# The first two weight sums of a seven-product matrix product: a VectorE addition against a plain load and an accumulating DMA

## Chip, core and metric

The kernel runs on one core of a Trainium2 chip. The metric is device time in microseconds (us): the median of several runs of the whole program. The engines are named as in the profile: PE (TensorE, matrix products; PEld are its weight loads), DVE (VectorE), ACT (ScalarE), POOL (GpSimd) and SP (SyncE, which here only issues DMAs). Weights, inputs and outputs lie in HBM; all work is done on tiles in SBUF, and products land in PSUM.

## What is computed

One inference step of a two-layer decoder trunk, for 512 prompt tokens and 8 x 4 sample tokens, 544 columns in all, with 1024 model channels. Every layer adds a token mixer and then a gated ConvFFN to the residual stream:

```python
for i in range(DEPTH):                       # 2 layers
    h = rms_norm(x, norm_mix[i])
    x = x + (conformer_conv if i == 0 else stick_breaking_attention)(h)
    h = rms_norm(x, norm_ffn[i])
    g = h @ w_gate                           # 1024 -> 2816
    g_conv = causal_dwconv(concat(past, g), w_dw, b_dw)      # width 3
    x = x + (silu(g_conv) * (h @ w_up)) @ w_down             # 2816 -> 1024
y = rms_norm(x, norm_final)
```

All inputs and outputs are float32. The change concerns weight matrices of 1024 rows, of which 256 columns are handled at a time: those of `w_gate` and `w_up` outside the first pass of each FFN, and half of the query matrix.

## The kernel before

**Products.** Each float32 product is made of three products of rounded operands: a weight tile W is split into a high half `whi` (ACT, L397, a cast) and a low half `wlo` (DVE, L400, W minus the high half); the data are split likewise into `XH` and `XL`. PE then adds whi x XH, whi x XL and wlo x XH in PSUM.

**Weights.** A raw tile (`raw`, 128 x 8 x 256 float32, 1 MB) holds 256 columns of a weight matrix: 8 blocks of 128 rows. There are two raw buffers; the load of the next but one is issued on SP (from the twelfth raw tile on; L360) as soon as the last split that reads the old one is emitted. The split pairs are kept in five slots (`SPLIT_BUFS`): slot s is written over slot s - 5, so a split can begin once PE is done with the fifth slot before it.

**Seven products for eight.** A "quad" is a raw tile seen as a 2 x 2 matrix of blocks of 512 rows x 128 columns, A11, A21 (the second 128 columns of the first 512 rows), A12 and A22, in the kernel's own naming; with the data also cut in two halves of 272 columns, seven block products and some additions give what eight would (Strassen's scheme in Winograd's form). It takes four slots, of kind 0, 2, 3 and 4: the plain first columns; the two sums in tile S; the third and fourth sums, which L1367 and L1369 write over the raw tile; and one plain block. `S[:, 0]` is A21 + A11 and `S[:, 1]` is A21 + A22: the two sums that this case is about. L1367 makes the third sum from `S[:, 1]`. Each of the seven block products is 12 matmuls of 128 x 272 (`products`, L1604 on). The data's own four sums are tiles TH and TL; `inputs` (L1460 on) makes them at the start of each FFN and uses the memory of S as scratch.

**S.** There is one S buffer per FFN (`pools["S"]`, L1448) and one for the query matrix (L1841). `sums` (L1353) takes it from a ring of one, so that a new pair of sums may be written only when every reader of the old pair is done: the high split, the low split, and L1367. 36 quads lie in the two FFNs, 2 in the query matrix.

**Order of the work.** Each FFN is planned as a whole: `plan.op` notes operations with an engine, an estimated cost and what they read (r) and write (w); `Plan.run` (L191) then simulates the engines and emits each engine's instructions in the order in which the simulation starts them. The emitted order is fixed; at run time each engine goes through its instructions in order and waits on semaphores. An operation on an engine name that does not exist (such as `raw5`) emits nothing and only holds back what depends on it, which is how the landing of a DMA is modelled. `used(slot)` (L1377) is called when the products of a slot are planned; it plans the split of the slot five further on, and, where that slot is of kind 2, the sums of its raw tile first.

**The FFN's passes.** The 22 chunks of 128 hidden channels go in passes of 4, 6, 6 and 6. The first pass is made of plain products. In each later pass come three gate quads with a down projection (the pass before, L1710) after each, the remaining down projections, and three up quads one behind the other; the first gate quad of the next pass follows at once. Gate products are copied (ACT, L1661) or added (DVE, L1666) into a tile G, whose columns for the samples' history POOL copies beforehand (L1541); POOL also copies the new state out of G (L1573, L1574) and issues its stores (L1728). L1564 is the convolution's multiply-add on DVE, L1716 the down projection's addition to the residual xT, L1865 and L1867 the evaluation of query quads. L2017 gathers cache pages by indirect DMA on POOL: 128 rows of 1024 float32 each.

Of the kernel before, what the change touches and what calls it, by code (L numbers as in the profile page):

```python
# [14 lines left out]
ALU = mybir.AluOpType  # L15
PSUM = bass.MemoryType.PSUM

P = 128
# [32 lines left out]
H_BUFS = 4  # L51
ACC_LATE = 5.5
U_POST = 1.0

WARM = (17, 29)
WARM_URGENT = 2.5
# [193 lines left out]
def tile_trunk(  # L250
# [8 lines left out]
    nc = tc.nc  # L259
    dve, act, pool, pe = nc.vector, nc.scalar, nc.gpsimd, nc.tensor  # L260
# [20 lines left out]
    raws = []  # L281
# [134 lines left out]
    W = Ring()  # L416
# [43 lines left out]
    def bank(tag, name):  # L460
        if tag == "tr" and "one" in banks:
            turns[0] += 1
            tag = "tr" if turns[0] % 3 else "one"
        return ps.tile([P, 512], F32, tag=tag, name=name, bufs=banks[tag])
# [3 lines left out]
    def uid(s):  # L468
        _n[0] += 1
        return f"{s}_{_n[0]}"  # L470
# [17 lines left out]
    def gemm(pt, st, slot, xh, xl, places=None, ks=(0, NF)):  # L488

        hi, lo, nk = W.w[slot]  # L490
        c0, n = st
        o = pt[:, :n]
        for k in range(max(0, ks[0]), min(nk, ks[1])):
            pe.matmul(o, hi[:, k, :], xh[:, k, c0:c0 + n], start=(k == 0), stop=False)
            pe.matmul(o, hi[:, k, :], xl[:, k, c0:c0 + n], start=False, stop=False)
            pe.matmul(o, lo[:, k, :], xh[:, k, c0:c0 + n], start=False, stop=(k == nk - 1))
            if places is not None and (k + 1) * 4 // nk > k * 4 // nk:
                for f in places[k * 4 // nk]:
                    f()
# [9 lines left out]
    def begin(n, ready, s0, st, xh, xl):  # L509

        pts = [bank("acc", uid("acc")) for _ in range(n)]
        for i, pt in enumerate(pts):
            gemm(pt, st, s0 + i, xh, xl, None, (0, ready))
        return pts
# [193 lines left out]
    for i in range(2):  # L708
        ch0 = (PE_CHUNKS[0] + i * len(PE_CHUNKS) // 2) * P
        for m in range(8):  # L710
            nj = min(4, CW - 4 * m)
            pool.dma_start(out=trow[i][m * n_g:(m + 1) * n_g, :nj * 32].rearrange("g (j h) -> g j h", j=nj),
                          in_=conv_w_dw[0, 4 * m:4 * m + nj, ch0:ch0 + n_g * 32].rearrange("j (g h) -> g j h", h=32))
# [4 lines left out]
    plan = Plan(E_CONV, 0.12, CONV_SHIFTS)  # L718
# [246 lines left out]
    blocks = [(xr[b], P, b) for b in range(4)] + [(xs, NS, 4)]  # L965
# [137 lines left out]
    for c in range(0, NC, 2):  # L1103
# [9 lines left out]
        for cc in range(2):  # L1113
            plan.op("act", 0.33, lambda c=c, cc=cc, pt=pt: act.copy(
                ext_s[:, c + cc, :, 0:PAST], pt()[:, cc * 240:(cc + 1) * 240].rearrange("p (b t) -> p b t", b=NB)),
                r=[pt, "junk"], w=[("past", c + cc)])
# [124 lines left out]
    for h, (c0, n) in enumerate(STREAMS):  # L1241
        if h:
            layer_norm(1)
        for g in (0, 4):
            for i in range(4):
                c = g + i
                pt = product(s0 + c, h)
                x = xT[:, c, c0:c0 + n]
# [3 lines left out]
        if not h:  # L1252
# [8 lines left out]
            r=[nrm.acc[0]], w=[ms])  # L1261
    plan.op("act", 0.34, lambda: act.activation(rs()[:, :n], ms()[:, :n], AF.Sqrt, bias=eps_t[:, 0:1], scale=1.0),
            r=[ms, "table"], w=[rs])
    plan.op("dve", 1.7, lambda: dve.reciprocal(rs()[:, :n], rs()[:, :n]), w=[rs])
    for c in range(NC):
# [3 lines left out]
                r=[rs, ("x", c, 0)], w=[u])  # L1269
# [4 lines left out]
            r=[u, ("XH", c, 0)], w=[("XL", c, 0)], lift=NLIFT)  # L1274
# [26 lines left out]
    def ffn(l, before, after):  # L1301
# [9 lines left out]
        plan = Plan(E_FFN)  # L1311
# [23 lines left out]
        def dcost(n):  # L1335
            return 0.06 + n * 1.06e-3

        def acost(n):
            return 0.04 + n * 0.885e-3
# [13 lines left out]
        def sums(r):  # L1353

            S = plan.tile("S", 1, lambda: pools["S"])
            S.after |= pools["inputs"]
            first = ("slot", s_of[r])

            def pair():
                x, s = W.raw[r], W.sums  # L1360
                s[r] = S()
                blocks = bass.AP(x.tensor, x.offset, [list(x.ap[0]), [4 * 2 * P + P, 2], [2 * P, 4], [1, P]])
                a21 = x[:, 0:4, P:]
                dve.tensor_tensor(S(), a21[:, None].to_broadcast([P, 2, 4, P]), blocks, op=ALU.add)

            plan.op("dve", dcost(1024), pair, r=[("raw", r)], w=[S])
            plan.op("dve", dcost(512), lambda: dve.tensor_tensor(  # L1367
                W.raw[r][:, 0:4, 0:P], S()[:, 1], W.raw[r][:, 0:4, 0:P], op=ALU.add), r=[("raw", r), S, first], w=[("S2", r)])
            plan.op("dve", dcost(512), lambda: dve.tensor_tensor(  # L1369
                W.raw[r][:, 4:, 0:P], W.raw[r][:, 0:4, 0:P], W.raw[r][:, 4:, 0:P], op=ALU.add), r=[first], w=[("S2", r)])  # L1370
            return S
# [5 lines left out]
        def used(slot):  # L1377

            s = slot + SPLIT_BUFS
            if ends and slot >= ends[0]:  # L1380
                if ends[0] + SPLIT_BUFS <= slot < ends[0] + NC:
                    return
                if slot < ends[0] + SPLIT_BUFS:
                    s = slot + NC
            if s >= len(specs):
                return
            r, kind, last, nk = specs[s]
            if kind == 0:
                s_of[r] = s
            if kind == 2:  # L1390
                live[r] = sums(r)
            prepare(s, [("slot", slot)])
# [160 lines left out]
        def smp(x, m, n):  # L1553
            return x[:, m:n].rearrange("p (b i) -> p b i", b=NB)
# [22 lines left out]
        def plain_pair(f2, s0, k0):  # L1577
# [16 lines left out]
            for i in range(2):  # L1594
# [3 lines left out]
                for c0, n in (SA, SB):  # L1598
                    plan.op("dve", dcost(n), lambda c0=c0, n=n, pt=ups[i, (c0, n)], h=h, s=sil[f]: dve.tensor_tensor(
                        h()[:, c0:c0 + n], s()[:, c0:c0 + n], pt()[:, :n], op=ALU.mult), r=[ups[i, (c0, n)], sil[f]], a=[h],  # L1600
                        urgent=U_POST)
                low_h(f, k0, h)
# [48 lines left out]
        def gate_quad(f2, slots):  # L1651
            g = [G(f2 + i) for i in range(2)]

            def put(what, p):
# [5 lines left out]
                if what[0] == "keep" or what[0] == "12":  # L1660
                    plan.op("act", acost(m), lambda: act.copy(dst(), p()[:, :m]), r=[p], w=[d], a=[g[i]], urgent=U_POST)  # L1661
                    if n > m:
                        plan.op("act", 0.2, lambda: act.copy(new(), smp(p(), m, n)), r=[p], w=[(*d, "s")], a=[g[i]], urgent=U_POST)
                    return
                op = SIGN[what[0]]
                plan.op("dve", dcost(m), lambda: dve.tensor_tensor(dst(), p()[:, :m], dst(), op=op),  # L1666
                        r=[p], w=[d], a=[g[i]], urgent=U_POST)
                if n > m:
                    plan.op("dve", 0.15, lambda: dve.tensor_tensor(new(), smp(p(), m, n), new(), op=op),
                            r=[p], w=[(*d, "s")], a=[g[i]], urgent=U_POST)  # L1670

# [5 lines left out]
        def low_h(f, k0, h):  # L1677
            plan.op("act", acost(T), lambda: act.copy(HH[:, f - k0, :], h()), r=[h], w=[("H", f - k0)])
            plan.op("dve", dcost(T), lambda: dve.tensor_tensor(
                HL[:, f - k0, :], h(), HH[:, f - k0, :], op=ALU.subtract), r=[h], w=[("H", f - k0)])  # L1680

        def up_quad(f2, slots, k0):
            hs = [buf(None, "h", [P, T], H_BUFS) for _ in range(2)]

            def put(what, p):
# [6 lines left out]
                if what[0] == "keep":  # L1692
                    plan.op("act", acost(n), lambda: act.copy(dst(), p()[:, :n]), r=[p], w=[d], a=[h], urgent=U_POST)
                    return
# [193 lines left out]
        s = first  # L1888
# [17 lines left out]
        if l == 0:  # L1906
            s = queries(s)
# [128 lines left out]
    def rows_q(j, bg):  # L2036
        rows = slice(j * HD, (j + 1) * HD)
        return rows, qT[rows, :, SEQ + 16 * bg:SEQ + 16 * bg + 16].rearrange("p c (b i) -> p c b i", b=4)
# [7 lines left out]
    for bg in range(2):  # L2046
        for j in range(2):
            rows, src = rows_q(j, bg)
# [28 lines left out]
    plan = Plan()  # L2077
# [433 lines left out]
    for i, tag in enumerate(("acc", "z", "z", "one")):  # L2511
# [3 lines left out]
        for q in range(4):  # L2515
            last = plan.op("pe", 6 * SA[1] * COL, weighted(pt, o0 + i, 0, q), w=[pt], follows=last,
                           r=[("slot", o0 + i)] + [("X", k) for k in (2 * q, 2 * q + 1)])
# [62 lines left out]
```

## Time and profile before

| what | value |
|---|---|
| time, median of 3 runs (lowest to highest) | 1270.66 us (1270.61 to 1270.97) |
| span of the profiled execution, first to last instruction | 1268.1 us |
| median less that span | 2.56 us |
| busy: PE, PEld, DVE, ACT, POOL | 1257.2, 1207.7, 1004.7, 717.5, 166.0 us |
| DMA traffic | 142.39 MB, mean 112 GB/s |
| DMA queue of SP (hardware descriptors) | 110350 packets, 111.89 MB, 28.2% of 16 engines' span |
| DMA queue of POOL (software descriptors) | 8704 packets, 28.80 MB, 7.0% |

The profile is of one execution; it names no time of its own beyond the span. Its rows are instructions with start and duration; a matmul's duration is longer than its spacing, since matmuls are pipelined, so PE's pace is read from counts in a window. Idle time before an instruction is put down to the semaphore event that ended it. DMA packets are traced apart from the instructions that issue them: "us to landing" runs from the issuing instruction to the last update of its semaphore, where that could be told. For SP's loads it could not, so their course is read from the share of the 16 DMA engines that is busy in narrow windows.

### The profile page before, as it was taken

The numbers are of one execution on the slowest core, as the hardware profiler recorded it, in microseconds if no ns is written. First come the engines' busy times: TensorE is split into PE (matmuls) and PEld (weight loads), VectorE is DVE, ScalarE is ACT, GpSimd is POOL, SyncE is SP. The second block draws the span as 40 slices with busy tenths as digits, with TensorE's granted clock in tenths as the row PEclk, the third lists the DMA queues.
The fourth block names the chain that finished last, engine by engine and source line by source line (L and its number), as shares of the span: only waits on it lengthen the run. The fifth ranks groups of instructions, "written<-read, shape, count | busy, mean of one in ns | idle before, by whom it ended". The sixth has DMA issues, their size and how long they took to land.

```text
span 1268.1 us, 26470 instructions
## 1 busy us (share of the span) xinstructions
PE 1257.2 (99%) x10846; PEld 1207.7 (95%) x10846; DVE 1004.7 (79%) x1696; ACT 717.5 (57%) x1436; POOL 166.0 (13%) x291
## 2 busy tenths in 40 slices
PE   9999999999999999999999999999999999999998
PEld 8997699999999999999989888999999999999998
DVE  7999876979987887869865589766988987886863
ACT  7794584635655455445564598754646645455453
POOL 5000014101001000002042143200111001000000
PEclk9999999999999999999999999999999999999999
DMA  7455423133233233244354443342123233232221
GB/s 221 131 165 156 119 69 115 35 100 102 92 112 99 74 112 115 62 144 172 116 185 154 152 144 132 119 145 73 62 85 117 91 96 117 67 119 91 85 77 72
DMA packets 119179, 142.39 MB, mean 112 GB/s; under 512 B 5101, under 2 KB 110245, under 8 KB 118786
## 3 DMA queue, kind: packets, MB, share of 16 engines
q1 hardware_dynamic: 110350, 111.89, 28.2%
q0 software_dynamic: 8704, 28.80, 7.0%
q8 instruction: 85, 1.39, 0.5%
q14 instruction: 36, 0.29, 0.1%
q10 hardware_dynamic: 4, 0.01, 0.0%
HBM read 129.34 MB, written 12.18 MB: 112 GB/s over the span
## 4 chain that ended last, share of the span: by engine, by line
PE 88%; DVE 9%; ACT 1%; issue 1%; DMA 0%; DVEq 0%; ACTq 0%
PE acc L1627 5%; PE acc L1626 5%; PE acc L1625 5%; PE acc L755 4%; PE acc L756 4%; PE acc L757 4%; PE av L892 3%; PE tr L1627 3%; PE tr L1626 3%; PE tr L1625 3%; PE av L1401 3%; PE av L1402 3%; PE av L1403 3%; PE tr L1401 3%; PE tr L1402 3%; PE tr L1403 3%
## 5 line engine op out<-in xcount | busy, mean ns | idle before, releaser
L397 ACT CAST whi<-raw 128x1024 fp32r<-128x1024 f32 (+2 forms) x247 | 224.3, 912 | 122.2 <-PE av L1402 25.1
L400 DVE TENSOR_TENSOR wlo<-raw,whi 128x1024 fp32r<-128x1024 f32 (+2 forms) x247 | 259.1, 1052 | 26.6 <-ACT whi L397 24.9
L755 PE MATMUL acc<-XH,whi 128*128 128x288 f32 (+1 forms) x384 | 112.7, 294 | 0.0
L757 PE MATMUL acc<-XH,wlo 128*128 128x288 f32 (+1 forms) x384 | 110.3, 287 | 0.9 <-DVE wlo L400 0.9
L756 PE MATMUL acc<-XL,whi 128*128 128x288 f32 (+1 forms) x384 | 110.3, 287 | 0.0
L1401 PE MATMUL av<-HH,whi 128*128 128x288 f32 (+1 forms) x280 | 83.3, 298 | 0.4 <-DVE xT L1716 0.4
L1627 PE MATMUL acc<-TH,wlo 128*128 128x272 f32 x288 | 83.0, 288 | 0.0
L1626 PE MATMUL acc<-TL,whi 128*128 128x272 f32 x288 | 82.7, 287 | 0.0
L1625 PE MATMUL acc<-TH,whi 128*128 128x272 f32 x288 | 82.7, 287 | 0.0
L1402 PE MATMUL av<-HL,whi 128*128 128x288 f32 (+1 forms) x280 | 82.6, 295 | 0.0
L2125 PE MATMUL acc<-XH,whi 128*128 128x256 f32 (+1 forms) x264 | 82.0, 311 | 0.6 <-ACT kT L2163 0.6
L1403 PE MATMUL av<-HH,wlo 128*128 128x288 f32 (+1 forms) x280 | 82.3, 294 | 0.0
L1661 ACT COPY G<-acc 128x272 f32<-128x272 f32 (+1 forms) x72 | 26.8, 372 | 94.7 <-PE acc L1627 94.7
L1401 PE MATMUL tr<-HH,whi 128*128 128x256 f32 (+1 forms) x280 | 79.1, 283 | 0.0
L1402 PE MATMUL tr<-HL,whi 128*128 128x256 f32 (+1 forms) x280 | 78.9, 282 | 0.0
L1403 PE MATMUL tr<-HH,wlo 128*128 128x256 f32 (+1 forms) x280 | 78.5, 280 | 0.0
L2127 PE MATMUL acc<-XH,wlo 128*128 128x256 f32 (+1 forms) x264 | 75.8, 287 | 0.0
L2126 PE MATMUL acc<-XL,whi 128*128 128x256 f32 (+1 forms) x264 | 75.8, 287 | 0.0
L755 PEld LDWEIGHTS acc<-XH,whi 128*128 128x128 f32 x384 | 72.2, 188 | 1.4 <-issue 0.4
L757 PEld LDWEIGHTS acc<-XH,wlo 128*128 128x128 f32 x384 | 72.1, 188 | 1.1 <-DVE wlo L400 1.1
L756 PEld LDWEIGHTS acc<-XL,whi 128*128 128x128 f32 x384 | 72.2, 188 | 0.3
L1564 DVE SCALAR_TENSOR_TENSOR cv<-G,fprm,cv 128x560 f32<-128x560 f32 x88 | 69.5, 797 | 0.5
(465 smaller groups left out, 4372.7 us busy)
## 6 DMA issues: line engine op xcount, KB each, us to landing
raw<-in_ffn_w_gate_dram SPq DMA_DIRECT2D x22, 1024.0 KB
raw<-in_ffn_w_up_dram SPq DMA_DIRECT2D x22, 1024.0 KB
raw<-in_ffn_w_down_dram SPq DMA_DIRECT2D x24, 768.0 KB
raw<-in_attn_w_qkv_dram SPq DMA_DIRECT2D x12, 1024.0 KB
raw<-in_conv_w_in_dram POOLq DMA_DIRECT2D x6, 1024.0 KB, 8.7
rep<-glu SPq DMA_DIRECT2D x36, 142.0 KB
raw<-in_conv_w_out_dram POOLq DMA_DIRECT2D x4, 1024.0 KB, 7.0
raw<-in_ffn_w_down_dram SPq DMA_DIRECT2D x8, 512.0 KB
```

What stands on the lines that cost most here:

```text
L397: act.copy(hi[:, k, :], src[:, k])
L400: dve.tensor_tensor(lo[:, k, :], src[:, k], hi[:, k, :], op=ALU.subtract)
L755: pe.matmul(o, hi[:, k, :], XH[:, k, c0:c0 + n], start=(k == 0), stop=False)
L756: pe.matmul(o, hi[:, k, :], XL[:, k, c0:c0 + n], start=False, stop=False)
L757: pe.matmul(o, lo[:, k, :], XH[:, k, c0:c0 + n], start=False, stop=(k == NC - 1))
L1401: pe.matmul(o, hi[:, j + k, :], xh, start=(start and k == 0), stop=False, **kw)
L1402: pe.matmul(o, hi[:, j + k, :], xl, start=False, stop=False, **kw)
L1403: pe.matmul(o, lo[:, j + k, :], xh, start=False, stop=(stop and k == len(xs) - 1), **kw)
L1625: pe.matmul(o, hi[:, j + k, :], xh, start=(start and k == 0), stop=False, **kw)
L1626: pe.matmul(o, hi[:, j + k, :], xl, start=False, stop=False, **kw)
L1627: pe.matmul(o, lo[:, j + k, :], xh, start=False, stop=(k == 3), **kw)
L2125: pe.matmul(o, hi[:, k, :], XH[:, k, c0:c0 + n], start=(k == 0), stop=False)
```

## The change

`pair`, the DVE addition that made both halves of S from the raw tile, is taken out. In its place SP loads A21 from HBM into both halves of S (two DMAs of 128 x 4 x 128 float32, 256 KB, in runs of 512 bytes), and POOL then adds A11 to the first half and A22 to the second by two DMAs with an accumulate operation, again read from HBM. The four new operations are planned in a chain, each writing S: `begin` on SP (0.9 us), a landing of `S_LAND` = 2.6 us, `add` on POOL (2.1 us), a landing of `S_ADDED` = 3.6 us. They do not depend on the raw tile; the raw tile is still loaded, for the other three slots. What reads S, and how, stays as it was.

```diff
@@ -51,6 +51,7 @@
 ACC_LATE = 5.5
 U_POST = 1.0
+S_LAND, S_ADDED = 2.6, 3.6

@@ -1355,15 +1356,21 @@
             S = plan.tile("S", 1, lambda: pools["S"])
             S.after |= pools["inputs"]
             first = ("slot", s_of[r])
-
-            def pair():
-                x, s = W.raw[r], W.sums
-                s[r] = S()
-                blocks = bass.AP(x.tensor, x.offset, [list(x.ap[0]), [4 * 2 * P + P, 2], [2 * P, 4], [1, P]])
-                a21 = x[:, 0:4, P:]
-                dve.tensor_tensor(S(), a21[:, None].to_broadcast([P, 2, 4, P]), blocks, op=ALU.add)
-
-            plan.op("dve", dcost(1024), pair, r=[("raw", r)], w=[S])
+            src = raws[r][0]
+
+            def begin():
+                W.sums[r] = S()
+                for i in range(2):
+                    nc.sync.dma_start(out=S()[:, i], in_=src[:, 0:4, P:])
+
+            def add():
+                for i in range(2):
+                    pool.dma_start(out=S()[:, i], in_=src[:, 4 * i:4 * i + 4, i * P:(i + 1) * P], accum_op=ALU.add)
+
+            plan.op("sp", 0.9, begin, w=[S])
+            plan.op(f"S{r}", S_LAND, lambda: None, w=[S])
+            plan.op("pool", 2.1, add, w=[S])
+            plan.op(f"S{r}", S_ADDED, lambda: None, w=[S])
             plan.op("dve", dcost(512), lambda: dve.tensor_tensor(
                 W.raw[r][:, 0:4, 0:P], S()[:, 1], W.raw[r][:, 0:4, 0:P], op=ALU.add), r=[("raw", r), S, first], w=[("S2", r)])
```

## The prediction

> **What bounds the kernel now.** I read the page's busy line and its chain first, then the windows by stage, then who TensorE waits for.
>
> ```profile
> span 1268.1 us, 26470 instructions
> PE 1257.2 (99%) x10846; PEld 1207.7 (95%) x10846; DVE 1004.7 (79%) x1696; ACT 717.5 (57%) x1436; POOL 166.0 (13%) x291
> ...
> PE 88%; DVE 9%; ACT 1%; issue 1%; DMA 0%; DVEq 0%; ACTq 0%
> ```
>
> TensorE (PE) is busy for 1257.2 of 1268.1 us, and 88% of the chain that ended last is its own work. The windows (length, then busy time of PE, its weight loads, DVE, ACT, POOL, then granted clock, DMA share, GB/s) show where the missing part lies:
>
> ```profile
> 200.00:270.00 70.00, 69.23 (x549) 68.35 (x548) 63.63 (x112) 37.43 (x76) 18.51 (x27) 1.00 0.22 73
> ...
> 350.00:450.00 100.00, 100.00 (x800) 100.00 (x799) 80.39 (x129) 49.27 (x85) 6.60 (x20) 1.00 0.31 96
> ...
> 540.00:640.00 100.00, 99.19 (x790) 98.60 (x789) 81.55 (x137) 52.00 (x94) 13.57 (x15) 1.00 0.43 144
> ...
> 880.00:940.00 60.00, 59.78 (x474) 59.22 (x473) 58.15 (x102) 34.66 (x66) 7.95 (x14) 1.00 0.24 78
> ```
>
> In 350 to 450, a stretch of seven-product quads, PE and its weight loads are busy for all 100 us at clock 1.00, while DVE has 19.6 us to spare. DVE is near its limit only at the two FFN starts (63.63 of 70, 58.15 of 60), and there PE loses 0.77 and 0.22 us; in the query stage it loses 0.81. Of the waits charged to DVE the largest are:
>
> ```profile
> PE acc L757 <- DVE wlo L400: 0.9, 1, 0.9
> ...
> PE av L1401 <- DVE xT L1716: 0.4, 2, 0.2
> ```
>
> So the kernel is bound by TensorE, and a lighter DVE can win back at most 0.77 + 0.22 + 0.81 = 1.8 us in the stages where the sums are made.
>
> **What is removed.** The pair addition L1364, once for each of 38 quads (durations are min/median/max in ns):
>
> ```profile
> L1364 DVE TENSOR_TENSOR S<-raw x36: 1215/1225/1228, 264.9 to 1193.6; 128x1024 f32<-128x1024 f32 x36
> ...
> L1364 DVE TENSOR_TENSOR Sq<-raw x2: 1217/1218/1218, 601.8 to 617.5; 128x1024 f32<-128x1024 f32 x2
> ```
>
> 36 x 1.225 + 2 x 1.218 = 46.5 us of DVE work go. PE's own work hides nearly all of it; what is late next is PE itself. Of the 1.8 us I credit only the 0.4 us that PE waited for the DVE additions L1716 at the FFN starts: **-0.4 us**. The wait of 0.9 us for wlo belongs to the group L757, the convolution stage's products, before any S is made. The bounds are 0 and -1.8.
>
> **What is added.** For each quad two plain loads of 256 KB on SP, and two accumulating DMAs of 256 KB on POOL, each waiting for its load: 38 x 1 MB more traffic beside 142. The sums no longer depend on the raw tile. They depend on S being free, and S is one buffer. It is read by the split of the second slot (ACT whi<-S, then DVE wlo<-S) and by L1367. So the new question is a loop: S free, load, accumulate, split, free again. Does it fit between one split and the next? In the run of quads without a down projection between them (three ups, then the next pass's first gate) the rows are:
>
> ```profile
> 303.01 1.03 ACT L397 CAST whi<-S 128x1024 fp32r<-128x1024 f32 x1
> ...
> 313.61 1.05 ACT L397 CAST whi<-S 128x1024 fp32r<-128x1024 f32 x1 [0.91 <-PE acc L1626]
> ...
> 324.13 1.05 ACT L397 CAST whi<-S 128x1024 fp32r<-128x1024 f32 x1 [0.70 <-PE av L1626]
> ...
> 334.70 1.05 ACT L397 CAST whi<-S 128x1024 fp32r<-128x1024 f32 x1 [0.51 <-PE tr L1626]
> ...
> 345.54 1.03 ACT L397 CAST whi<-S 128x1024 fp32r<-128x1024 f32 x1
> ```
>
> ```profile
> 304.88 1.22 DVE L400 TENSOR_TENSOR wlo<-S,whi 128x1024 fp32r<-128x1024 f32 x1
> ...
> 315.09 1.22 DVE L400 TENSOR_TENSOR wlo<-S,whi 128x1024 fp32r<-128x1024 f32 x1
> ...
> 325.73 1.22 DVE L400 TENSOR_TENSOR wlo<-S,whi 128x1024 fp32r<-128x1024 f32 x1
> ...
> 336.59 1.22 DVE L400 TENSOR_TENSOR wlo<-S,whi 128x1024 fp32r<-128x1024 f32 x1
> ...
> 347.88 1.22 DVE L400 TENSOR_TENSOR wlo<-S,whi 128x1024 fp32r<-128x1024 f32 x1
> ```
>
> S is free at 306.10, 316.31, 326.95 and 337.81 (start plus 1.22) and is read again at 313.61, 324.13, 334.70 and 345.54. The gaps are 7.51, 7.82, 7.75 and 7.73, together **30.8 us for four refills**. The pair addition filled such a gap with 1.2 us. If a refill takes R, each split comes R - 7.7 later than the one before it, and the delay adds up over four quads.
>
> How much delay PE forgives: the fourth split ends at 349.10, and PE first uses that slot here:
>
> ```profile
> 352.64 0.29 PE L1625 MATMUL acc<-TH,whi 128*128 128x272 f32 x1
> ```
>
> That is 3.5 us. PE can also take one product of plain inputs ahead, 12 matmuls of 100/800 = 0.125 us: 1.5 us. The room is 5.0 us, and the point from which it decides is 4R - 30.8 = 5.0, **R = 8.95 us**.
>
> **What a refill costs.** No row shows an accumulating DMA. The nearest rows are one 512 KB load on SP with the DMA share around it, the POOL DMAs with KB each and us from issue to landing, and the POOL instructions that issue them:
>
> ```profile
> 264.06 0.37 SPq L360 DMA_DIRECT2D raw<-in_ffn_w_down_dram  x1
> ```
>
> ```profile
> 265.00:266.00 1.00, 1.00 (x10) 0.98 (x9) 1.00 (x2) 0.24 (x2) 0.47 (x1) 1.00 0.64 191
> 266.00:267.00 1.00, 1.00 (x8) 0.79 (x7) 1.00 (x3) 0.00 (x0) 0.65 (x2) 1.00 0.96 334
> 267.00:268.00 1.00, 1.00 (x8) 1.00 (x9) 0.97 (x2) 0.00 (x0) 0.00 (x0) 1.00 0.12 36
> ```
>
> ```profile
> raw<-in_conv_w_in_dram POOLq DMA_DIRECT2D x6, 1024.0 KB, 8.7
> ...
> xT<-in_cache_k_dram,idx POOLq DMA_INDIRECT x16, 5.6
> ...
> out_dram<-h POOLq DMA_DIRECT2D x6, 6.0 KB, 3.8
> ```
>
> ```profile
> L1728 POOL DMA_DIRECT2D out_dram<-h x16: 522/561/635, 265.5 to 1219.2; - x16
> ```
>
> ```profile
> L360 POOL DMA_DIRECT2D raw<-in_conv_w_in_dram x6: 884/886/932, 20.7 to 68.8; - x6
> ```
>
> The 512 KB load, issued at 264.06, has the last of its packets just after 267: 3.1 us. Two loads of 256 KB carry the same bytes in packets half as long and one issue of 0.37 more; I take 3.3. The two adds write 512 KB. The gather moves 128 rows of 4 KB, also 512 KB, and lands 5.6 us after issue; the second add is issued 0.56 to 0.89 after the first, I take 0.7. So R = 3.3 + 5.6 + 0.7 = **9.6 us**. The lower end is 3.1 + 3.8 + 0.56 = 7.5, as if an add were as cheap as the 6 KB store. The upper end is 3.3 + 8.7 + 0.9 = 12.9, as if 1 MB were moved, because the adds must also read S, and the next raw load shares the engines. I take 9.6 because the gather row has the same bytes.
>
> At 9.6 the fourth split is 4 x 9.6 - 30.8 = 7.6 us late, 2.6 more than the room. The second FFN is built by the same function and has the same run: 2 x 2.6 = **+5.2 us**. Shorter runs stay inside: two quads give 2 x (9.6 - 7.7) = 3.8, under 5.0. Where a down projection lies between, the gap is wider still.
>
> **Starts of the FFNs.** S is a scratch tile of the input sums until then, and the plan lets the first loads begin after the last of them:
>
> ```profile
> 262.07 1.36 DVE L1484 TENSOR_TENSOR TL<-cv,TH 128x544 fp32r<-128x544 f32 x2
> 263.34 0.69 DVE L400 TENSOR_TENSOR wlo<-raw,whi 128x512 fp32r<-128x512 f32 x1
> ```
>
> ```profile
> 275.93 0.29 PE L1625 MATMUL acc<-TH,whi 128*128 128x272 f32 x1
> ```
>
> The last low half there (263.34) also releases the raw load at 264.06, on the same SP queue. If the S loads stand behind it, their packets start after 267.1 and land about 2.0 later, at 269.1; the adds land 6.3 on, at 275.4; the split takes 1.05 + 1.22, to 277.7. PE needs that slot at 275.93 and its low half 0.25 later: 1.5 us late. If SP takes the S loads first, nothing is late. I take 1.0 for each FFN, **+2.0 us**; the ends are 0 and 3.0, and each us on R adds one per start.
>
> **POOL's queue.** An add that waits for its load holds what is behind it in order: the copies of the convolution's history into G (L1541), for which ACT's G copies wait. These two rows are the last such copy before a gate quad's output, and that output:
>
> ```profile
> 294.89 0.20 POOL L1541 COPY G<-fprm 128x16 f32<-128x16 f32 x1 [1.87 <-DVE cv L1564]
> ```
>
> ```profile
> 298.69 0.36 ACT L1661 COPY G<-acc 128x240 f32<-128x240 f32 x1 [0.99 <-PE acc L1627]
> ```
>
> The cover is 3.6 us (294.89 + 0.20 to 298.69). The longest hold is the load's 3.3 and two issues, 1.4: at worst 1.1 us for each of 18 gate quads, 20 us in all. I cost it at 0, because the plan orders POOL by the time at which the loads should have landed. SP waits for S before it issues, and behind it stand only raw loads whose release (a later split) comes after that of S: 0. ACT and DVE stand in order behind a late split, with the copies out of PSUM; that is inside the lateness above.
>
> **The sum.** -0.4 + 5.2 + 2.0 = +6.8 us. The profiled execution would span 1268.1 + 6.8 = 1274.9. The median of the timed runs is 1270.66, 2.56 more than that span, for what lies around the instructions; I keep it: **1277.5 us**.
>
> **Rivals.** (1) *The refill is hidden*: R stays under 8.95 us, and no split is late enough. For it: 30.8 us in four gaps, and 7.5 as the lower end. Against it: the adds wait for the loads, so two DMA latencies stand in a row, and only the 6 KB stores land in 3.8. Time: 1270.66, less up to 1.8: 1268.9 to 1273.2, where the FFN starts alone cost up to 3.0. Measurement tells 0.2% (2.5 us) from no change, so this is no change. By the Trainium skill, page DMA: Bandwidth & Descriptors, section "Anatomy of one DMA — SWDGE (gpsimd) path", a POOL DMA takes about 2.0 us plus its bytes at 436 GB/s; two such steps of 256 KB would make the refill about 6 us and give this rival's time. The trace disagrees: 1 MB lands in 8.7 us, where that rule gives 4.4.
>
> (2) *The adds run at half rate, or beside the raw load*: R = 12.9. Runs of four: 2 x (4 x 12.9 - 30.8 - 5.0) = 31.6. Runs of two, one in each FFN: 2 x (2 x 5.2 - 5.0) = 10.8. Starts: 2.0 + 2 x 3.3 = 8.6. Less 0.4: +50.6, 1321. For it: the raw load of the same quad runs at a share near 1 for some 3 us right after S is freed:
>
> ```profile
> 321.46 0.37 SPq L360 DMA_DIRECT2D raw<-in_ffn_w_up_dram  x1
> ```
>
> ```profile
> 323.00:324.00 1.00, 1.00 (x10) 1.00 (x9) 0.97 (x2) 0.42 (x2) 0.00 (x0) 1.00 0.79 216
> 324.00:325.00 1.00, 1.00 (x10) 1.00 (x9) 0.96 (x3) 0.87 (x1) 0.00 (x0) 1.00 1.09 387
> ```
>
> Against it: shares of 0.31 over the stage leave room.
>
> (3) *The freed DVE decides*: 46.5 us of additions gone let the plan place the rest better. Place: the FFN starts and the queries; price: at most -1.8, so 1268.9; it would need R under 8.95 as well, and over 2.5 us only by a luckier order elsewhere. The change does what it says: the two slices added are those that the addition read.
>
> **How the numbers follow.** Forecast (1273.3 to 1292, R from 9.2 to 11): 0.46. Rival 1: 0.30. Rival 2, from 1292 up: 0.18. Rival 3, below 1268.1: 0.06. Faster by over 0.2%: 0.06; within: 0.30; slower: 0.64. The likeliest case's own range is 1273 to 1292. The range is 1268.6 to 1306: it leaves out rival 3's tail and the upper two thirds of rival 2, together under 0.2.
>
> **What would show it.** Right: whi<-S waiting for a DMA on S, growing through u0, u1, u2 and the next gate; PE idle near 350 and near 275, and at the like places of the second FFN; DVE down by 46 us. The add landing 5 to 7 us after issue is the step on which most hangs. Wrong: splits at the old times with S landed before them (R under 8.95); PE waiting for G behind POOL; or PE idle in every quad, so that R is over 13.

## The result: 50 us slower

| | before | changed |
|---|---|---|
| time, median (lowest to highest) | 1270.63 us (1269.91 to 1270.97) | 1320.36 us (1315.52 to 1323.23) |
| span of the profiled execution | 1268.1 us | 1320.1 us |
| ratio of the times, 95% interval | | 1.0391 (1.0376 to 1.0405) |

The changed kernel is 49.7 us slower. The forecast was 1277.5 us and its range ended at 1306: the measured time lies above both. The second rival, a refill of 12.9 us, had given 1321.

The page of the changed kernel, span and busy times, then the two DMA queues, then the chain that ended last, by engine and by line:

```profile
span 1320.1 us, 26799 instructions
...
PE 1274.5 (97%) x10846; PEld 1218.7 (92%) x10846; DVE 964.6 (73%) x1658; ACT 717.0 (54%) x1436; POOL 265.1 (20%) x367
...
q1 hardware_dynamic: 150478, 131.82, 32.6%
q0 software_dynamic: 48832, 48.72, 19.0%
...
PE 22%; DMA 6%; DVE 5%; issue 1%; ACT 1%; POOL 0%; DVEq 0%; POOLq 0%; ACTq 0%; SPq 0%
DMA S<-in_ffn_w_up_dram 3%; DMA S<-in_ffn_w_gate_dram 2%; PE acc L1632 2%; PE acc L1634 2%; PE acc L1633 2%; PE acc L495 2%; PE acc L496 2%; PE acc L497 2%; DVE wlo L401 1%; PE av L1408 1%; PE av L1409 1%; PE av L1410 1%; PE tr L1408 1%; PE tr L1409 1%; PE tr L1410 1%
```

DVE's busy time fell by 40.1 us. The prediction's sign was 46: the durations of DVE's instructions do add up to 46.0 us less, but busy time counts overlaps once. But transfers into S now stand in the chain (6%), where DMA had 0% before. POOL's queue has 48,832 packets where it had 8,704.

The splits of S in the first run of back-to-back quads (ACT's timeline; start, duration, in brackets the idle time ahead and what ended it):

```profile
306.00 1.06 ACT L398 CAST whi<-S 128x1024 fp32r<-128x1024 f32 x1
...
322.12 1.04 ACT L398 CAST whi<-S 128x1024 fp32r<-128x1024 f32 x1 [3.97 <-DMA S<-in_ffn_w_up_dram]
...
335.74 1.05 ACT L398 CAST whi<-S 128x1024 fp32r<-128x1024 f32 x1 [5.40 <-DMA S<-in_ffn_w_up_dram]
...
349.75 1.05 ACT L398 CAST whi<-S 128x1024 fp32r<-128x1024 f32 x1
...
364.30 1.05 ACT L398 CAST whi<-S 128x1024 fp32r<-128x1024 f32 x1 [3.70 <-DMA S<-in_ffn_w_gate_dram]
```

From split to split it takes 16.1, 13.6, 14.0 and 14.6 us; before it was 10.6, 10.5, 10.6 and 10.8. ACT waits for S to land, and it waits in order. What follows the split of 322.12 on ACT, and what then releases PE:

```profile
323.07 0.35 ACT L1668 COPY G<-acc 128x240 f32<-128x240 f32 x1
323.32 0.19 ACT L1670 COPY G<-acc 128x32 f32<-128x32 f32 x1
```

```profile
323.56 0.40 PE L1632 MATMUL acc<-XH,whi 128*128 128x272 f32 x1 [1.42 <-ACT G L1670]
```

These two copies empty a PSUM bank. They had nothing to do with S, and stood behind the split that waited for it. PE stands still again, for 2.69 us, behind the split of 335.74, there too for a copy; only at the split of 364.30 does it wait for the halves of S themselves, for 0.72 and 1.29 us. So the list of PE's waits names copies on ACT, not S (us in total, times, longest):

```profile
PE acc L1632 <- ACT G L1668: 7.0, 4, 3.3
PE tr L1632 <- ACT h L1700: 5.1, 2, 2.7
PE av L1632 <- ACT h L1700: 5.1, 3, 3.3
PE acc L1634 <- DVE wlo L401: 3.3, 4, 1.3
PE acc L1410 <- DVE wlo L401: 3.3, 2, 1.6
```

One step further back, in the waits of ACT and DVE, stands the transfer:

```profile
ACT whi L398 <- DMA S<-in_ffn_w_up_dram: 33.9, 9, 6.0
DVE raw L1374 <- DMA S<-in_ffn_w_up_dram: 28.7, 10, 6.1
ACT whi L398 <- DMA S<-in_ffn_w_gate_dram: 26.6, 8, 4.6
DVE raw L1374 <- DMA S<-in_ffn_w_gate_dram: 26.0, 9, 4.8
```

**Where the 51 us arose.** All these kernels run the same 10,846 matmuls. I took the start of the n-th matmul in each trace and subtracted that of the n-th matmul of before; where this difference grows, time is lost. The columns are stretches of the kernel before: the two FFN starts (250 to 300, 900 to 980 us), the two runs of four quads (300 to 380, 980 to 1060), the two runs of two (420 to 480, 1100 to 1140), the query stage (580 to 700) and the rest. R is a refill of S, from the issue of its first load to the landing of its second add (where the trace has no landing, the last packet plus 0.33 us), median of 38. The runs other than the changed kernel are explained below.

| kernel | R, us | starts | runs of four | runs of two | query | rest | all |
|---|---|---|---|---|---|---|---|
| changed | 12.4 | 3.1, 3.1 | 12.2, 15.8 | 3.1, 7.1 | 3.7 | 3.3 | 51.4 |
| plain_adds | 10.7 | 2.2, 2.8 | 4.8, 8.1 | 1.3, 1.9 | 1.5 | 1.4 | 24.0 |
| raw_kept | 10.3 | 2.2, 2.3 | 5.5, 4.7 | 1.7, 1.3 | 4.0 | 0.6 | 22.2 |
| both_short | 8.1 | 2.8, 2.8 | 1.1, 1.1 | 0.0, 0.0 | 1.5 | 0.4 | 9.5 |
| two_s | 12.9 | 4.3, 7.7 | 0.0, 0.0 | 0.0, 0.0 | 0.3 | 1.0 | 13.2 |
| two_old | 12.8 | -0.2, -0.2 | 0.0, 0.0 | 0.0, 0.0 | 0.0 | -0.1 | -0.5 |
| two_first | 12.6 | -0.8, -0.8 | 0.0, 0.0 | 0.0, 0.0 | 0.3 | 0.5 | -0.9 |
| true_costs | 12.2 | 3.4, 3.1 | 18.1, 17.7 | 4.9, 9.8 | 6.2 | 0.5 | 63.9 |
| old_costs | 12.6 | -0.4, -0.4 | 23.5, 20.7 | 10.4, 10.6 | 9.5 | 12.2 | 86.0 |

### The profile page after: what moved, and what is told of

Read it like the earlier page. It is cut to its first block, busy times and chain, and to the rows that moved or that the text cites. A ratio compares the mean times of both kernels' runs of the same rounds, so it can differ in the third digit from the quotient of the medians.

```text
span 1320.1 us, 26799 instructions
## 1 busy us (share of the span) xinstructions
PE 1274.5 (97%) x10846; PEld 1218.7 (92%) x10846; DVE 964.6 (73%) x1658; ACT 717.0 (54%) x1436; POOL 265.1 (20%) x367
## 3 DMA queue, kind: packets, MB, share of 16 engines
q0 software_dynamic: 48832, 48.72, 19.0%
## 5 line engine op out<-in xcount | busy, mean ns | idle before, releaser
L1410 PE MATMUL av<-HH,wlo 128*128 128x288 f32 (+1 forms) x280 | 82.5, 295 | 0.0
L1410 PE MATMUL tr<-HH,wlo 128*128 128x256 f32 (+1 forms) x280 | 78.6, 281 | 0.0
L398 ACT CAST whi<-S 128x1024 fp32r<-128x1024 f32 x36 | 37.8, 1050 | 66.5 <-DMA S<-in_ffn_w_up_dram 33.9
```

Of the source, the lines that this page charges most:

```text
L398: act.copy(hi[:, k, :], src[:, k])
L1410: pe.matmul(o, lo[:, j + k, :], xh, start=False, stop=(stop and k == len(xs) - 1), **kw)
```

## The experiments

Theory A was the loop through the one S buffer: S free, load, accumulate, split, free again, at 12.4 us a refill against gaps of 7.7 us. Rivals were the traffic itself, the plan's order, and the in-order wait on ACT.

### Two buffers (two_s), and the control (one_s_h3)

```diff
-H_BUFS = 4
+H_BUFS = 3
-            S = plan.tile("S", 1, lambda: pools["S"])
+            k = len(plan.rings.get("S", [])) % 2
+            S = plan.tile("S", 2, lambda: pools["S"] if k == 0 else pools["S1"])
...
+                pools["S1"] = pools["t"].tile([P, 2, 4, P], F32, name=f"S1{l}")
```

The control has only the first two lines. Expected of two_s:

> The changed kernel with a second buffer for S (a ring of two), and room for it made by a ring of 3 in place of 4 for the hidden tiles (H_BUFS). A refill may then begin a whole quad earlier: about 7.7 + 10.5 = 18 us lie between the last read of one buffer and the next first read of it, against 10 to 15.5 us that refills take in the trace of after. Theory A (what costs is the loop through the one S buffer): the losses in the runs of quads go (about 12 + 16 + 3 + 7 = 38 us of the 50), the 6 us of the two FFN starts stay, perhaps 4 us of the query stage: 1276 to 1284 us. Theory B (1 MB more traffic for each quad, packets of the adds that hold up the raw loads, and an add that holds up POOL): the traffic and the queues are the same, so 1308 to 1325 us. Theory C (the plan's order alone: S chains ranked differently): near 1300 to 1320 as the costs it is given are the same.

Of one_s_h3:

> The changed kernel with one S buffer as it is, and only the ring of hidden tiles cut from 4 to 3: the control for the run with two buffers. Every theory expects it within 6 us of the changed kernel, 1314 to 1326 us.

Measured: two_s 1283.7 us, ratio to before 1.0107 (1.009 to 1.0124); one_s_h3 1317.48 us, 1.037 (1.0349 to 1.0391). With two buffers the runs of quads lose nothing, to a tenth of a microsecond, with the same transfers on the same queues. Theory A holds for the runs, and theory B falls: 1 MB more for each quad costs no time by itself. Theory C, the order of the plan alone, had given 1300 to 1320 and falls too. Of the 13.2 us that are left, 12.0 arise at the FFN starts; why they lose more there than with one buffer (4.3 and 7.7 against 3.1 each) was not examined.

### The same transfers with no reader (dummy), and its control (before_h3)

```diff
+                plan.op("dve", 0.07, lambda: dve.tensor_copy(pools["D"][:, :, 0, 0:1], S()[:, :, 3, P - 1:P]),
+                        r=[S, ("slot", slot)], w=["D"])
+                plan.op("sp", 0.9, begin, w=["D"])
...
+                plan.op("pool", 2.1, add, w=["D"])
```

> The kernel before, with its pair addition on VectorE, and beside it the same four transfers for each quad (two plain loads on SP, two accumulating ones on POOL) into a tile D that nothing reads; they start when the split of S is through, as in the changed kernel (a copy of two columns on VectorE, about 0.1 us for each quad, ties them to it). Ring of hidden tiles 3. No split waits for these transfers. Theory A: within 5 us of the kernel before with a ring of 3, 1270 to 1277 us. Theory B (traffic, contention with the raw loads, an occupied POOL queue): 1295 to 1320 us.

> The kernel before with the ring of hidden tiles cut from 4 to 3: the control for the run with the unread transfers. Both theories: 1269 to 1275 us.

Measured: dummy 1296.56 us, 1.0213 (1.0196 to 1.023); before_h3 1270.92 us, 1.0005 (0.9996 to 1.0015). I had expected 1270 to 1277 of the dummy, so this is a miss, but one of the experiment's design. Its waits:

```profile
DVE S L1381 <- DMA raw<-in_ffn_w_gate_dram: 13.3, 12, 3.1
DVE D L1361 <- DMA D<-in_ffn_w_up_dram: 12.5, 8, 4.1
DVE D L1361 <- DMA D<-in_ffn_w_gate_dram: 7.0, 4, 3.1
```

The tiny copy that starts the transfers writes D, and so waits until the transfers before it have landed: I had built the same loop again, this time with DVE in it (19.5 us of waits in the last two rows). In the first row the pair addition waits for a raw tile that comes late; why it was late was not followed up. The run cannot be read as a price of traffic, since two_old and two_first below carry the same traffic at no cost.

### The plan's order at the FFN starts (two_old, two_first)

two_old tells the plan the old cost, in two_s:

```diff
-            plan.op("sp", 0.9, begin, w=[S])
-            plan.op(f"S{r}", S_LAND, lambda: None, w=[S])
-            plan.op("pool", 2.1, add, w=[S])
-            plan.op(f"S{r}", S_ADDED, lambda: None, w=[S])
+            plan.op("sp", 0.0, begin, w=[S])
+            plan.op("pool", 0.0, add, w=[S])
+            plan.op(f"S{r}", dcost(1024), lambda: None, w=[S])
```

two_first keeps the costs and frees the first sum of each FFN from the input sums, in two_s:

```diff
-            S = plan.tile("S", 2, lambda: pools["S"] if k == 0 else pools["S1"])
-            S.after |= pools["inputs"]
+            S = plan.tile("S", 2, lambda: pools["S1"] if k == 0 else pools["S"])
+            S.after |= pools["inputs"] if k else {pools["op"]}
```

> Two buffers for S as in the run before (1283.7 us), but the plan is told that a sum costs what the addition on VectorE cost (SP 0, POOL 0, 1.15 us until it lands) in place of 0.9 + 2.6 + 2.1 + 3.6 us. Theory A1 (the 13.2 us that are left with two buffers are an order of the plan: the longer chain of S gives the input sums a higher rank at the two FFN starts, so VectorE makes them ahead of the low halves that TensorE needs next): the starts come back, 1270 to 1275 us. Theory B1 (the starts lose because the first refill itself comes late): 1281 us or more, as the splits are now also placed too early.

> Two buffers for S, the plan's costs as in the changed kernel, but the first sum of each FFN goes into the buffer that is no scratch tile of the input sums, so its load waits only for the pool of the sums to open and not for the last input sum. Theory A1 (order of the plan): the input sums lose the high rank that they had through the wait of the first S, 1270 to 1276 us. Theory B1 (late refill): the first refill is early here as well, so also 1270 to 1276 us; together with the run with the old costs this tells them apart. If neither holds, it stays at 1281 to 1286 us.

Measured: two_old 1270.31 us, 1.0 (0.999 to 1.0009); two_first 1269.48 us, 0.9995 (0.9986 to 1.0005). Each cures both starts and equals before. In two_old the first pair of sums lands at 266.5 us, no earlier than in the changed kernel (266.3), and the start still loses nothing. That speaks for the order of the plan (A1) and against the late refill (B1). The order can be read on DVE, here in the changed kernel and then in before:

```profile
250.03 0.72 DVE L1491 TENSOR_TENSOR TL<-cv,TH 128x544 fp32r<-128x544 f32 x1
250.78 0.72 DVE L1487 TENSOR_TENSOR cv<-cv,XH 128x544 f32<-128x544 f32 x1
...
252.12 0.72 DVE L1487 TENSOR_TENSOR cv<-cv,XL 128x544 f32<-128x544 f32 x1
252.76 1.22 DVE L401 TENSOR_TENSOR wlo<-raw,whi 128x1024 fp32r<-128x1024 f32 x1
```

```profile
244.19 1.21 DVE L400 TENSOR_TENSOR wlo<-raw,whi 128x1024 fp32r<-128x1024 f32 x1
...
257.26 0.72 DVE L1484 TENSOR_TENSOR TL<-cv,TH 128x544 fp32r<-128x544 f32 x1
...
258.23 0.72 DVE L1480 TENSOR_TENSOR cv<-cv,XH 128x544 f32<-128x544 f32 x1
```

The first S waits for the input sums, so a longer chain behind S makes the input sums more urgent to the plan. It moved them some 7 us forward, and the low half that PE needs next, made at 244.19 before, came at 252.76. That is the wait of PE for wlo at L1410 in the list above, 1.6 us at each start. The rest of the 3.1 us that a start loses is, at the first, two more waits (0.7 us for G, 0.6 for h), and at the second 1.5 us in a stretch of half clock that follows the stall (last section).

two_first, its busy line and its window of 350 to 450:

```profile
PE 1256.7 (99%) x10846; PEld 1207.6 (95%) x10846; DVE 962.9 (76%) x1658; ACT 720.1 (57%) x1436; POOL 268.2 (21%) x367
```

```profile
350.00:450.00 100.00, 100.00 (x800) 100.00 (x799) 72.29 (x120) 49.02 (x84) 22.99 (x32) 1.00 0.68 161
```

PE is busy for all 100 us with 800 matmuls, as in before, with refills that still take 12.6 us and with DMA at a share of 0.68 in place of 0.31.

### What a refill is made of (plain_adds, raw_kept, both_short)

plain_adds takes the accumulation away, so that S lacks A21 (one buffer, costs as in the changed kernel):

```diff
-                    pool.dma_start(out=S()[:, i], in_=src[:, 4 * i:4 * i + 4, i * P:(i + 1) * P], accum_op=ALU.add)
+                    pool.dma_start(out=S()[:, i], in_=src[:, 4 * i:4 * i + 4, i * P:(i + 1) * P])
```

raw_kept leaves out the raw loads of both FFNs, so that the adds meet no other load (a part of its edit):

```diff
...
+            if self.nraw in kept:
+                self.raw[self.nraw] = self.tiles[self.nraw] = self.tiles[self.nraw - RAW_BUFS]
+                self.nraw += 1
+                return
...
```

> The changed kernel with the two transfers on POOL as plain loads, without the accumulation: the sums leave out the term that is added to both slices (the block A21). Same bytes written, same waits, same queues. Theory E (the accumulation is what makes a refill long: its 512-byte packets take 66 ns where plain ones take 27, 1024 of them on 16 engines, 64 x 39 ns = 2.5 us): a refill of about 9.9 in place of 12.4 us, a run of four quads 4 x 2.5 = 10 us shorter, two such runs, and 3 to 5 us from each run of two: 1285 to 1300 us. Theory F (a refill is long because its packets wait behind the raw load's, and two landings stand in a row, whatever the kind of transfer): 1310 to 1322 us.

> The changed kernel with one S buffer, with the raw loads of both FFNs left out: each quad finds in its raw tile what an earlier one left there, so its slots other than the sums are of wrong weights. All transfers for S stay as they are. Theory G (part of a refill is waiting behind the raw load that is issued about when the adds are: refills take 10.1 us where under 0.3 MB of other loads run beside them, 13.2 where over 0.8 MB do): refills of about 10 us, 2.4 shorter; the runs of four save about 4 x 2.4 each, the runs of two 3 to 5 each, the queries nothing: 1287 to 1300 us. Theory H (that link is by chance, and the adds' own packets set the time): refills stay at 12 us or more, 1310 to 1322 us.

Measured: plain_adds 1290.05 us, 1.0153 (1.0136 to 1.0169); raw_kept 1290.71 us, 1.0156 (1.014 to 1.0171). Both theories E and G hold, each for about 30 us. raw_kept also spares ACT the waits of its splits for raw tiles, 11.4 us in the changed kernel; that its runs of four lose what the shorter R gives (5.4 us, below) speaks for R as the cause, but no run took the two apart. The DMA table (KB each, median us from issue to landing), changed kernel first, then plain_adds with its POOL queue, then raw_kept:

```profile
S<-in_ffn_w_gate_dram POOLq DMA_DIRECT2D x36, 256.0 KB, 7.7
...
S<-in_ffn_w_up_dram POOLq DMA_DIRECT2D x36, 256.0 KB, 6.6
```

```profile
S<-in_ffn_w_gate_dram POOLq DMA_DIRECT2D x36, 256.0 KB, 6.1
...
S<-in_ffn_w_up_dram POOLq DMA_DIRECT2D x36, 256.0 KB, 4.7
```

```profile
q0 software_dynamic: 14784, 48.72, 12.7%
```

```profile
S<-in_ffn_w_gate_dram POOLq DMA_DIRECT2D x36, 256.0 KB, 4.7
...
S<-in_ffn_w_up_dram POOLq DMA_DIRECT2D x36, 256.0 KB, 5.1
```

plain_adds moves the same 48.72 MB in 14,784 packets where the changed kernel needs 48,832: for the two adds of a quad 128 packets of about 220 ns in place of 1,024 of about 66 ns. On 16 engines that is 8 x 0.22 = 1.8 us against 64 x 0.066 = 4.2. The measured R is 1.7 us shorter.

How the raw load gets in the way is seen in the changed kernel's windows (length; busy PE, PEld, DVE, ACT, POOL; clock, DMA share, GB/s). The adds were issued from 312.26, the raw load at 312.66; S landed at 322.0:

```profile
315.00:316.00 1.00, 1.00 (x11) 1.00 (x10) 0.77 (x5) 0.92 (x2) 0.04 (x1) 1.00 1.04 370
316.00:317.00 1.00, 1.00 (x11) 1.00 (x10) 1.00 (x2) 0.00 (x0) 0.00 (x0) 1.00 1.09 368
...
318.00:319.00 1.00, 1.00 (x11) 1.00 (x10) 0.00 (x0) 0.15 (x1) 0.00 (x0) 1.00 1.44 191
319.00:320.00 1.00, 1.00 (x11) 1.00 (x10) 0.00 (x0) 0.00 (x0) 0.00 (x0) 1.00 1.49 180
```

First 370 GB/s, which is the raw load, and only then 180 to 190, which is the adds in their small packets. The packets of this add begin 5.1 us after its issue. In raw_kept they begin a median of 1.99 us after it; over the changed kernel's 38 refills it is 2.0 to 5.1. DVE and ACT meanwhile do next to nothing (318 to 320).

both_short has both edits at once.

> Both shortenings at once, one S buffer: plain loads on POOL in place of the accumulating ones (the sums leave out the block A21) and the raw loads of both FFNs left out (slots of wrong weights). Refills of about 8.2 us are expected, as in the run with plain loads where under 0.3 MB ran beside them. Theory A (a run of n back-to-back quads loses n x R less the gaps of 7.7 us each, less the room of 5.0 us, and nothing where that is below zero): the decision point for a run of four is R = 8.95, so at 8.2 the runs of four and of two lose nothing; the starts (4 to 6 us) and up to 4 us of the query stage stay: 1274 to 1281 us. Theory K (each refill costs in proportion, with no point below which it is hidden: one saves 30 us and the other 30 us, so both save what is there): also about 1270, but with losses left inside the runs of four at 300 to 380 and 980 to 1060 of over 2 us each. If the two savings overlap (the accumulation matters only because of the raw load): 1285 to 1291 us.

Measured: 1279.57 us, 1.0073 (1.0057 to 1.009), R 8.1 us. The prediction had put the point of decision for a run of four at R = 8.95. Below it the runs of four lose 1.1 us each and the runs of two nothing; what is left is the starts (5.6), the query stage (1.5) and 0.4. Theory K asked for over 2 us left in each run of four, so it falls. In R the two savings add up (1.7 and 2.1 us alone, 4.3 together). In time they do not (30, 30 and 41 us), since below the point of decision nothing is left to save.

### What the plan believes (true_costs, old_costs)

Both have one S buffer. true_costs sets `S_ADDED` from 3.6 to 7.0; old_costs has the edit of two_old.

> The changed kernel with one S buffer; only the plan is told 7.0 us in place of 3.6 us for the landing of the adds, near what the trace shows (6.6 and 7.7 us). Theory A (the loop through the one buffer is the bound in runs of quads: a refill takes what it takes): little comes back, 1308 to 1325 us. Theory D (much of the loss is that ACT, in its written order, waits for S with copies out of PSUM behind the wait, which a truer plan would put in front): 1290 to 1306 us.

> The changed kernel with one S buffer; the plan is told that a sum costs what the addition on VectorE cost (SP 0, POOL 0, 1.15 us). Theory A with A1 (the starts lose by the plan's order, the runs by the loop through S): the 6 us of the two starts come back, the runs lose as before or a little more, because the splits are placed earlier and what stands behind them on ACT and VectorE waits longer: 1308 to 1325 us. If the plan's order were most of the loss it would be under 1295 us.

Measured: true_costs 1332.98 us, 1.0484 (1.0466 to 1.0501); old_costs 1354.48 us, 1.0648 (1.0627 to 1.0669). Both are slower than the changed kernel, and both miss all that I had expected: theory D is wrong even in its sign, and theory A gave too little for both. The waits of PE, true_costs first:

```profile
PE acc L1634 <- DVE wlo L401: 6.8, 8, 1.9
PE av L1634 <- DVE wlo L401: 6.5, 4, 2.2
```

```profile
PE tr L1631 <- ACT h L1699: 23.8, 6, 5.3
PE av L1631 <- ACT h L1699: 20.5, 6, 5.5
```

R hardly moves (12.2 and 12.6 us), so it is the place of the split that counts. Told that S is late, the plan puts the split late, and PE waits for the low half itself (11.3 us for low halves of S). Told that S is early, it puts the split early, and PE waits for 44 us for copies of h that stand behind it on ACT. One of these waits, on ACT and then on PE:

```profile
352.81 1.04 ACT L398 CAST whi<-S 128x1024 fp32r<-128x1024 f32 x1 [8.00 <-DMA S<-in_ffn_w_up_dram]
353.76 0.38 ACT L1699 COPY h<-av 128x272 f32<-128x272 f32 x1
```

```profile
354.19 0.60 PE L1631 MATMUL av<-XH,whi 128*128 128x272 f32 x1 [5.50 <-ACT h L1699]
```

Two such waits, of 3.4 us each, lie outside the stretches of the table and are part of the 12.2 us in its column "rest". A part of both losses is the clock of the last section: while it is half, PE falls 16.5 us behind in true_costs and 21.4 in old_costs, against 9.1 in the changed kernel. In old_costs the starts lose nothing (-0.4 each), which settles A1 with one buffer too. So theory A gets a second half: the loop sets how late S is, and the written order sets how much of it PE forgives. Why 3.6 us does better than both was not examined further.

### Both cures at once (two_best)

two_first with the costs of two_old, to see whether the freed DVE is worth anything.

> Two buffers for S, the first sum of each FFN in the buffer that is no scratch tile, and the plan's old costs: both cures of the starts at once. What is left is the gain of 46 us of VectorE work gone, which the prediction put at 0.4 us, with 1.8 as the most. Theory I (TensorE is the bound, so nothing is to be had): 1268.5 to 1271.5 us. Theory J (the freed VectorE lets more work come early): under 1267.5 us.

Measured: 1272.21 us, 1.0017 (1.0008 to 1.0026); a little slower than two_first alone. It also misses the range of theory I, which ended at 1271.5. In its trace 2.0 us are lost in the query stage, where PE waits 1.1 us for DVE's evaluation into qT. No version beat before by more than can be measured; theory J falls.

## Why the prediction was wrong

**PE is the bound; a lighter DVE brings 0.4 us, 1.8 at the most: right.** With the loop and the starts cured, 40 us less on DVE gave 1270.31 us against 1270.31, and 1269.48 in the better of two.

**The loop through S, and the sum 4R - 30.8 - 5.0: the loop right, the sum near, in part by luck.** The sum was tried at four values of R, for each run of four: at 12.4 it gives 13.8, measured 12.2 and 15.8; at 10.7, 7.0 (4.8 and 8.1); at 10.3, 5.4 (5.5 and 4.7); at 8.1 nothing (1.1 and 1.1). But PE does not lose as the sum has it, once, behind the fourth split: it stops at splits before that, for copies that the prediction had put "inside the lateness above", and the 12.2 and 15.8 us hold 3.1 and 1.5 us of half clock, for which the sum has no term. The room of 5.0 us belongs to the order that the plan wrote: the runs of true_costs and old_costs lose 18 and 22 us at about the same R.

**R = 9.6 us: this is the step that failed, by size.** Without the raw load beside it a refill takes 10.3 (3.3 + 0.7 + 5.6 were taken; 3.5 + 0.8 + 5.4 to 6.4 are usual in raw_kept). In the changed kernel it takes 12.4, and the 2.1 us between are the raw load. The prediction had seen it and quoted its rows, but had put it into a rival with a chance of 0.18. What it set against that rival was a stage mean, a DMA share of 0.31. That is the wrong measure: the release of S and that of the raw tile lie a few us apart (308.77 and 312.66 in the run shown), so the raw load meets the adds, whatever the mean: in 26 of 38 refills over 0.8 MB of other loads ran beside the adds. The gather, from which 5.6 came, also was the wrong neighbour for packets: it moves rows of 4 KB, where the adds move 512 bytes at a time. That its 5.6 us comes near the 5.4 to 6.4 of raw_kept is luck.

**Runs of two stay inside: wrong, by the same size.** 2 x (12.4 - 7.7) - 5.0 = 4.4 us; measured 3.1 and 7.1.

**FFN starts +2.0, for S behind the raw load: wrong mechanism.** They cost 6.2 us, by the plan's order on DVE. The first S loads were issued at 247, and the first split of S waited for PE and not for S:

```profile
273.96 1.05 ACT L398 CAST whi<-S 128x1024 fp32r<-128x1024 f32 x1 [0.93 <-PE tr L1409]
```

Nothing in the trace of before can show this. But the plan's rule, which starts what is most urgent, stood in the code, and the change put 9.2 us into a chain where 1.15 had been.

**POOL and SP at 0: right**, as two_old shows with the same queues. The query stage, which the sum left out, lost 3.7 us.

With R = 12.4 the prediction's own sum, and the starts and the query as measured, is 2 x 13.8 + 2 x 4.4 + 6.2 + 3.7 - 0.4 = 45.9 us of the 51.4; 3.3 are spread over the rest. This is a check of size and no more, as the half clock is in the measured figures and not in the sum. The range was too narrow at the top because it cut the second rival off, though its end of R, 12.9, was one that the prediction had named itself. That the rival's 1321 us was met so closely is in part luck: it too charged the starts to a late S.

## What to carry to other kernels

When an operation on an idle engine is replaced by transfers, count the buffers before the bytes: a latency of 12 us was free with two buffers and cost some 38 us in the runs of quads with one. Bound a transfer by what runs beside it at that moment in each turn of the loop, not by the mean share of the stage. And a planner's costs are part of the change: a longer chain raises the rank of all that feeds it, also of work that has nothing to do with the transfer.

## What the hardware showed that was not expected

**The accumulating DMA moves small packets.** The same 256 KB into the same tile went in packets of 512 bytes with accumulation and in an eighth as many without it, on the same queue (48,832 against 14,784 packets in all).

**A transfer that was issued first can move last.** The adds' packets began up to 5.1 us after the issue while a raw load issued 0.4 us after the first of them (and 0.9 us before the second) ran at 370 GB/s. By the Trainium skill, page DMA: Bandwidth & Descriptors, section "Queues, rings and completion order", each DMA engine takes turns between its queues, packet by packet. By that rule alone the adds should have begun beside the raw load. The windows do not show it: the rate falls from 370 to 190 GB/s only when the raw load ends. Whether the adds' descriptors were late or their packets were held was not tried.

**A short stall can cost twice.** In the changed kernel PE idles for 2.0 us between 364.7 and 367.2 us, at the end of the run of four, and then runs at a lower granted clock (the column before the DMA share):

```profile
366.00:367.00 1.00, 0.00 (x0) 0.00 (x0) 1.00 (x2) 1.00 (x2) 0.00 (x0) 1.00 0.00 0
...
369.00:370.00 1.00, 1.00 (x5) 0.84 (x4) 1.00 (x3) 0.83 (x2) 0.00 (x0) 0.50 1.14 343
370.00:371.00 1.00, 1.00 (x6) 1.00 (x6) 1.00 (x2) 0.00 (x0) 0.05 (x1) 0.50 0.44 99
371.00:372.00 1.00, 1.00 (x7) 1.00 (x7) 1.00 (x2) 0.11 (x1) 1.00 (x2) 0.60 0.75 187
```

Some 3.4 us at half clock follow; a microsecond of this view has 5 to 7 matmuls in place of the 10 or 11 that it counts at full clock. It is seen six times in the changed kernel, after 1.6 to 3.3 us of idle PE. By the starts of the n-th matmuls PE falls 1.5 to 1.7 us further behind in each, 9.1 us of the 51 together. The link is no fixed one: a stall of 1.63 us that began at 943.4 was followed by such a stretch, one of the same length at 252.4 and one of 2.45 us at 1025.4 were not. PE's busy time agrees in kind: 17.3 us more for the same matmuls. The Trainium skill, page TensorE: Matmul & The Clock Gate, section "Part 1: The HAM clock gate", tells of a clock that is either full or half, by activity in windows of about 3.4 us; the trace agrees with both numbers. Each of the six stretches has clock 0.5 and lasts 3.41 us. By the same section of the Trainium skill the clock falls after at least one idle window of about 3.4 us. In this trace less idle time, 1.6 to 3.3 us, was enough. No run took the clock apart from the stalls that bring it about.
